# One output tile of a batched product stored by sixteen transfers in place of one

## The chip, the cores and the metric

The kernel runs on one core of a Trainium2 chip. Its time is the device time of one execution in microseconds (us), lower is better: the median of the runs before is 300.16 us. The profile is of one such execution. Five compute and control engines appear in it: PE (TensorE, matrix products), ACT (ScalarE), DVE (VectorE), POOL (GpSimd) and SP (SyncE, which here only issues transfers). Besides these there are 16 DMA engines, which move the bytes between the chip's main memory and the on-chip memory; a transfer is split over them.

## What is computed

For each of 96 (batch, head) pairs the kernel multiplies a 512 x 64 matrix by the transpose of another:

```python
x: (8, 12, 512, 64) float32
y: (8, 12, 512, 64) float32
np.einsum('bhtc,bhsc->bhts', x, y).astype(np.float32)   # (8, 12, 512, 512)
```

It reads 25.17 MB and writes 100.66 MB, so four bytes in five are results.

## The kernel before

The 96 pairs are taken in six groups of 16 (`NG`). An input of a group, 2 MB of float32, is one transfer: 128 rows (partitions) of 16 KB. There are twelve such loads (`load`, line 142), x and y in turn. The results leave in 48 output tiles (`V * NH`), each 2 MB as well: 128 partitions of `K * S` = 8 x 512 float32, which is 16 KB each. In main memory a tile is not one block: it is seen as 64 x 2 rows (`q`, `u` in the view `ov`, lines 55 to 57), two blocks of 64 rows of 16 KB; row `q` of block `u` lies in partition `2q + u`.

Loads and stores share five buffers of 2 MB, `slots`, given out in turn (`slot`, line 138). A slot that holds a result is free for the next one when its store has landed.

The inputs are turned to bfloat16 and rearranged: `compress` (line 151) copies a loaded slot on ACT, DVE and POOL, `mix` (line 174) gathers pieces of x, and `transposes` (line 189) makes the transposed operands on DVE. TensorE runs a loop over all output tiles (`all_products`, line 223); a tile is two halves of four products each, one half in each of two accumulators `pm`. `result` (line 241) copies the two halves from `pm` into a slot, on ACT for every tile but the last, and then calls `store` (line 237).

All order between engines is written out by hand. `emit` (line 113) works out which semaphores an operation has to wait for, gives the waits to its engine ahead of it, and lets the operation raise a semaphore when it is done. Each slot has a semaphore of its own for transfers (`dma0` to `dma4`); a transfer raises it by 16 in all when every part has landed. `need` (line 73) leaves out a wait that the engine has already made. Who next writes into a slot waits for the full count of the transfers that read it.

Every transfer is issued by SP, in the order of the program: first five loads, then the rest of the loads and the first stores as slots come free, and from the twelfth load on only stores. A store is issued as soon as the second half of its tile is in the slot. SP's queue is in order, so whatever stands behind an issue waits for it.

At the end of the program POOL waits for all semaphores, last of all for the last store's, and clears them.

Of the kernel before, what the change touches and what calls it, by code (L numbers as in the profile page):

```python
# [9 lines left out]
def kernel(  # L10
# [22 lines left out]
    nc = tc.nc  # L33
    B, H, T, C = x.shape
    _, _, S, _ = y.shape
# [7 lines left out]
    K = 8  # L43
    E = R // K
    D = 32
    SLOTS = 5
    fp32 = mybir.dt.float32
    bf16 = mybir.dt.bfloat16
    u32 = mybir.dt.uint32
# [5 lines left out]
    ov = out.rearrange("b h t s -> (b h t s)").rearrange(  # L55
        "(o u h q n) -> o h q u n", u=2, h=V, q=Q * E, n=K * S
    )

    def buffer(name, width, dtype):
        return nc.alloc_sbuf_tensor(name, [P, width], dtype)[:, :]  # L60

    slots = [buffer(f"slot{i}", K * S, fp32) for i in range(SLOTS)]
    xks = [buffer(f"xk{i}", R * C, bf16) for i in range(NG - 1)]
# [9 lines left out]
    def need(name, points, told=True):  # L73

        best = {}
        for p, v in points:
            if known[name].get(p, 0) < v:
                best[p] = max(best.get(p, 0), v)
        for p, v in list(best.items()):
            if any(snaps[q, w].get(p, 0) >= v for q, w in best.items() if q != p):  # L80
                del best[p]
        for p, v in best.items():
            if told:
                engines[name].wait_ge(sems[p], v)  # L84
            known[name][p] = v
            for q, w in snaps[p, v].items():
                known[name][q] = max(known[name].get(q, 0), w)

    def promise(name, reads, writes):

        points = [writer[r] for r in (*reads, *writes) if r in writer]
        points += [v for w in writes for v in readers.get(w, ())]
        if name == "pool" and name in ticks:
            points.append((name, ticks[name]))
        return points

    def record(name, p, step, reads, writes, queue=False):
        at = (p, ticks.get(p, 0) + step)
        ticks[p] = at[1]
        if not queue:  # L100
            own[name][p] = at[1]
        snaps[at] = {**known[name], **own[name], p: at[1]}
        for r in reads:
            readers.setdefault(r, []).append(at)
        for w in writes:
            writer[w], readers[w] = at, []

    def signal(p):
        if p not in sems:
            sems[p] = nc.alloc_semaphore(p)  # L110
        return sems[p]

    def emit(name, make, reads=(), writes=(), dma=None, by=None, step=1):
        need(name, promise(name, reads, writes))
        p = by or name
        if dma is not None:
            p, step = f"dma{dma}", 16
        make().then_inc(signal(p), step)
        record(name, p, step, reads, writes, dma is not None)
# [15 lines left out]
    def both(i):  # L135
        return [("slot", i, 0), ("slot", i, 1)]

    def slot():
        made_slots.append(len(made_slots) % SLOTS)
        return made_slots[-1]  # L140

    def load(n):
        i = loaded[n] = slot()
        emit(
            "sp",
            lambda: nc.sync.dma_start(slots[i], (yv if n % 2 else xv)[n // 2]),  # L146
            writes=both(i),
            dma=i,
        )
# [86 lines left out]

    def store(o, s):
        i, h = divmod(o, V)
        emit("sp", lambda: nc.sync.dma_start(ov[i, h], slots[s]), reads=both(s), dma=s)

    def result(o, s):

        ot = slots[s].rearrange("p (r s) -> p r s", s=S)
        for k in range(0, K, 4):
            pm = k // 4
            half = o // V % 2
            reads, writes = [("xT", half), ("yT", half)], [("pm", pm)]
            signal("pe")
            need("pe", promise("pe", reads, writes), told=False)
            record("pe", "pe", 1, reads, writes)  # L250
            copy(
                "dve" if o == V * NH - 1 else "act", ot[:, k:k + 4, :], pms[pm],
                [("pm", pm)], [("slot", s, pm)], by=f"free{pm}",
            )
        store(o, s)
# [9 lines left out]
    with tc.tile_critical():  # L265
        for n in range(SLOTS):
            load(n)
# [12 lines left out]
    for n in range(2 * NG):  # L280
# [6 lines left out]
        if n < 5:  # L287
            load(n + SLOTS)
        elif n in (6, 8):
# [52 lines left out]
```

## Time and profile before

| | |
|---|---|
| median of three runs | 300.16 us (300.13 to 300.43) |
| the profiled execution | 300.31 us |
| its span, first to last instruction | 298.2 us |
| transfers | 12 loads and 48 stores of 2048 KB each |
| bytes | 25.17 MB read, 100.66 MB written, 422 GB/s over the span |
| ACT busy | 208.0 us (70%) |
| DVE busy | 156.4 us (52%) |
| PE busy | 140.3 us (47%) |
| POOL busy | 56.1 us (19%) |
| SP: issue of a store | 0.54 us median, 48 of them |
| store, from issue to landing | 20.8 us median |

The page cuts the span into 40 equal slices, one digit for the busy share in tenths. "Idle before" and "waited for" name what released an engine. The chain of work that ended last is followed back from the end of the program. The trace also holds every DMA packet (start, duration, size) and every arrival at a semaphore; a packet's record doesn't say which of the 16 DMA engines moved it.

Tile 20, which the change touches, is issued as a store at 144.7 us and has landed at 165.6 us.

### The profile page before, as it was taken

How to read it: one execution, taken by the hardware profiler on the slowest of the kernel's cores; microseconds unless marked ns; L12 is line 12 of the kernel's file. 1: busy time of each engine (PE TensorE's matmuls, PEld its weight loads, DVE VectorE, ACT ScalarE, POOL GpSimd, SP SyncE). 2: the span in 40 equal slices, each digit the busy share in tenths (PEclk: the TensorE clock that was granted, in tenths of full speed). 3: DMA queues.
4: the chain of work that ended last, by engine and by line, in shares of the span. 5: the costliest groups of instructions: out<-in, count | busy, mean ns of one | idle time of the engine just before them, and what ended most of it. 6: DMA issues, size and time to landing. Idle time of an engine off the chain costs nothing.

```text
span 298.2 us, 1225 instructions
## 1 busy us (share of the span) xinstructions
PE 140.3 (47%) x384; PEld 36.5 (12%) x384; DVE 156.4 (52%) x75; ACT 208.0 (70%) x107; POOL 56.1 (19%) x23
## 2 busy tenths in 40 slices
PE   0000040548556655747566746666746656656000
PEld 0000010111111111111111111111111111111000
DVE  2257897999839592916809449076093430002300
ACT  1665576999999988686868686868676777774000
POOL 2399999991000000000000000000000000000000
PEclk9999999996799997595676595677596677596555
DMA  7999999999999999999999999999999999999996
GB/s 275 429 426 440 424 431 424 426 435 431 431 426 437 426 431 432 431 431 431 433 429 434 429 433 426 433 429 435 429 429 424 424 431 429 424 426 429 426 426 288
DMA packets 8642, 125.85 MB, mean 422 GB/s; under 512 B 960, under 2 KB 960, under 8 KB 960
## 3 DMA queue, kind: packets, MB, share of 16 engines
q1 hardware_dynamic: 8640, 125.83, 99.2%
q14 instruction: 2, 0.02, 0.0%
HBM read 25.17 MB, written 100.66 MB: 422 GB/s over the span
## 4 chain that ended last, share of the span: by engine, by line
DMA 62%; ACT 22%; issue 4%; DVE 3%; PE 1%; SPq 0%; ACTq 0%; DVEq 0%
DMA out_dram<-slot 48%; ACT slot L127 20%; DMA slot<-in_y_dram 7%; DMA slot<-in_x_dram 6%; DVE yb L129 2%; DVE slot L129 2%; PE pm L217 1%; ACT xk L127 1%; ACT yb L127 1%; SPq L146 0%; ACTq L84 0%; SPq L269 0%; DVEq L84 0%; SPq L265 0%
## 5 line engine op out<-in xcount | busy, mean ns | idle before, releaser
L217 PE MATMUL pm<-yT,xT 128*128 128x512 bf16 x384 | 140.3, 513 | 133.9 <-ACT slot L127 97.2
L127 ACT ACTIVATE slot<-pm 128x2048 f32<-128x2048 f32 x94 | 170.5, 1891 | 42.4 <-DMA out_dram<-slot 40.5
L194 DVE STREAM_TRANSPOSE xT<-xb 128x2048 uint32<-128x2048 uint32 x12 | 46.8, 3896 | 69.9 <-PE pm L217 67.5
L217 PEld LDWEIGHTS pm<-yT,xT 128*128 128x128 bf16 x384 | 36.5, 116 | 237.1 <-ACT slot L127 150.4
L129 DVE COPY xb<-xk 32x2048 bf16<-32x2048 bf16 x36 | 46.9, 1304 | 1.0
L129 DVE CAST yb<-slot 64x2048 bf16<-64x2048 f32 x12 | 36.2, 3019 | 13.1 <-DMA slot<-in_y_dram 12.9
L129 POOL COPY xb<-xk 32x2048 bf16<-32x2048 bf16 x12 | 36.2, 3020 | 6.6 <-ACT xk L127 5.9
L127 ACT ACTIVATE xk<-slot 128x4096 bf16<-128x4096 f32 x6 | 21.7, 3617 | 12.5 <-DMA slot<-in_x_dram 12.5
L203 DVE STREAM_TRANSPOSE yT<-yb 128x1024 uint32<-128x1024 uint32 x12 | 23.1, 1924 | 0.0
L129 DVE COPY slot<-pm 128x2048 f32<-128x2048 f32 x2 | 4.5, 2287 | 32.9 <-DMA out_dram<-slot 32.9
L127 ACT ACTIVATE yb<-slot 64x2048 bf16<-64x2048 f32 x6 | 14.8, 2462 | 5.1 <-DMA slot<-in_y_dram 5.1
L129 POOL CAST yb<-slot 64x2048 bf16<-64x2048 f32 x6 | 17.8, 2969 | 1.3 <-DMA slot<-in_y_dram 0.8
L127 ACT ACT_TABLE_LOAD x1 | 1.3, 1283 | 4.5 <-PEq L269 4.5
L276 DVE MEMSET xb<- 128x2048 uint32 x1 | 1.8, 1765 | 5.0 <-PEq L269 5.0
L276 POOL MEMSET xb<- 128x2048 uint32 x1 | 1.8, 1804 | 4.1 <-POOLq L269 4.1
L326 POOL MEMSET const-float32-0.0<- 128x1 f32 x1 | 0.1, 98 | 0.2 <-issue 0.2
L326 POOL MEMSET const-float32-1.0<- 128x1 f32 x1 | 0.1, 98 | 0.0
L326 POOL MEMSET const-bfloat16-1.0<- 128x1 bf16 x1 | 0.1, 98 | 0.0
L326 POOL MEMSET const-uint8-127<- 128x1 uint8 x1 | 0.1, 98 | 0.0
## 6 DMA issues: line engine op xcount, KB each, us to landing
out_dram<-slot SPq DMA_DIRECT2D x48, 2048.0 KB, 20.8
slot<-in_x_dram SPq DMA_DIRECT2D x6, 2048.0 KB, 17.5
slot<-in_y_dram SPq DMA_DIRECT2D x6, 2048.0 KB, 20.8
```

The source lines that it names most:

```text
L127: lambda: nc.scalar.activation(dst, src, COPY)
L129: else engines[name].tensor_copy(dst, src),
L194: lambda: nc.vector.transpose(xTs[half].rearrange("p (k r e) -> p k e r", k=K, e=E), xbs[half].rearrange("p (k e c) -> p k e c", k=K, e=E),),
L203: lambda: nc.vector.transpose(yTs[half].rearrange("p (r j) -> p j r", r=D), ybs[half][b].rearrange("p (j c) -> p j c", c=D),),
L217: last = nc.tensor.matmul(pms[k // 4][:, j, :], xT[:, k + j, h, :], yT[:, h * S:(h + 1) * S], start=True, stop=True,)
L276: lambda: engines[name].memset(xbs[half], 0.0),
L326: nc = _bacc.Bacc("TRN2", target_bir_lowering=False, num_devices=1)
```

## The change

```diff
+    N = K * S
+    UNEVEN = 20
...
     def store(o, s):
         i, h = divmod(o, V)
-        emit("sp", lambda: nc.sync.dma_start(ov[i, h], slots[s]), reads=both(s), dma=s)
+        if o != UNEVEN:
+            emit("sp", lambda: nc.sync.dma_start(ov[i, h], slots[s]), reads=both(s), dma=s)
+            return
+        cut = N - S
+        parts = [(ov[i, h][:, :, :cut], slots[s][:, :cut])]
+        for u, counts in enumerate(((15, 14, 13, 12, 10), (11, 9, 8, 7, 6, 5, 4, 3, 3, 8))):
+            q = 0
+            for n in counts:
+                parts.append((ov[i, h][q:q + n, u, cut:], slots[s][2 * q + u:2 * (q + n - 1) + u + 1:2, cut:]))
+                q += n
+        for dst, src in parts:
+            emit("sp", lambda: nc.sync.dma_start(dst, src), reads=both(s), dma=s)
```

47 of the 48 stores stay as they are. Tile 20 is stored by sixteen transfers, issued one after another on SP's queue where the one stood: first the leading 14 KB of all 128 rows (3584 of 4096 float32), then the last 2 KB (512 float32) of each row, by fifteen transfers. Five of them have the 64 rows of block 0, in runs of 15, 14, 13, 12 and 10 rows; ten have the 64 rows of block 1, in runs of 11, 9, 8, 7, 6, 5, 4, 3, 3 and 8. Row `q` of block `u` is read from partition `2q + u`, so a run takes every second partition. All sixteen raise the semaphore of the same slot, and the next writer of the slot waits for all of them. The bytes stored are the same, and nothing is changed on the compute engines but the count in that wait. The purpose as stated is that DMA engines of a high number move less.

## The prediction

> **What bounds the kernel now.** I read the page's DMA rows first, then the queue table, the chain, the rows of the store issue, and last the trace's packet records.
>
> ```profile
> DMA  7999999999999999999999999999999999999996
> DMA packets 8642, 125.85 MB, mean 422 GB/s; under 512 B 960, under 2 KB 960, under 8 KB 960
> q1 hardware_dynamic: 8640, 125.83, 99.2%
> DMA 62%; ACT 22%; issue 4%; DVE 3%; PE 1%; SPq 0%; ACTq 0%; DVEq 0%
> out_dram<-slot SPq DMA_DIRECT2D x48, 2048.0 KB, 20.8
> ```
>
> The 16 DMA engines are busy in every slice but the first and last: 99.2% of sixteen engines' span. No compute engine is above 70%. There are 60 transfers of 2 MB; 8,640 packets are 60 x 16 x 9, so on each DMA engine a transfer is eight rows of 16 KB and one 4-byte completion write (the 960 small ones).
>
> The chain in order of time (start, us, what) shows a loop from 126 us on:
>
> ```profile
> 129.93 20.85 DMA out_dram<-slot
> ...
> 150.86 3.65 ACT slot L127 x2
> ...
> 154.53 20.85 DMA out_dram<-slot
> ```
>
> and the timeline has the copies into the split store's slot, waiting for its landing:
>
> ```profile
> 165.64 3.65 ACT L127 ACTIVATE slot<-pm 128x2048 f32<-128x2048 f32 x2 [1.29 <-DMA out_dram<-slot]
> ```
>
> A store lands 20.85 us after its issue, ScalarE refills the slot in 3.65 us, and the store five later is issued. In 20.85 us four transfers are in the queue (20.85 / 4.92), so the DMA engines are never out of work. The loop follows them; it doesn't set their pace.
>
> What ends the span is finer than the page. The packet records (start, duration, size; no engine number) and the semaphore arrivals show sixteen streams. A 16 KB packet is recorded with 611 ns and the next begins 607 ns after it; a 4-byte one with 9 ns and the next begins 6 ns later. Fifteen streams need 8 x 607 + 6 = 4,862 ns a transfer (first arrivals 85.71 to 110.02 for five). One stream, followed back from its last packet at 297.66 to 115.84, has no gap and takes 181.82 / 37 = 4.914 us a transfer: about half of its packets take 614 to 644 ns. The arrivals of a store's sixteen completions (us) show it falling behind:
>
> ```
> store  issued   1st     15th    16th    16th after 1st
>  4      78.20   86.11   86.59   86.69   0.57
> 20     144.71  163.87  165.00  165.56   1.69
> 30     193.88  212.58  213.49  214.77   2.19
> 47     278.36  296.03  296.57  298.14   2.10
> ```
>
> The span ends at 298.2, right behind that one arrival, 1.57 us after all others. So the end is set by the sum of one DMA engine's packets. It lies in mid-field at 61 us and loses some 60 ns a transfer from there, so its slowness belongs to the engine, not to a place in the order. The trace doesn't say which number it has.
>
> **The change, part by part.** Store 20, one transfer of 128 rows x 16 KB, becomes one of 128 rows x 14 KB and fifteen with 128 pieces of 2 KB between them. By the change's description high numbers move less; I cost it so that a transfer of n rows gives a piece to each of the n lowest engines. Counting which of the fifteen sizes exceed e, engines 0 to 15 get 15, 15, 15, 13, 12, 11, 10, 9, 7, 6, 5, 4, 3, 2, 1, 0 pieces (128), where before each had eight. [...] No trace here shows it yet.
>
> Removed from every engine: 2 KB of eight packets. 14 KB is not in the trace; on the line between the 8 KB instruction packets (309 ns) and 16 KB (611) it is 309 + 302 x 6/8 = 535.5 ns, pitch 531. Saved: 8 x 76 = 0.61 us. Bounds: 0 (a fixed packet price) to 8 x 302 = 2.4 (an 8 KB price); I take the line, since two sizes lie on it.
>
> Added: a 2 KB packet and a completion write for each piece. On the line from the 32-byte packets (7 ns) to 8 KB (309), 2 KB is 82 ns, pitch 78, and 6 for the write: 84 ns. Bounds: 6 + 6 ns and 309 + 6 ns; I take 84, as 2 KB is eight times the completion's time or more by bytes alone (611 / 8 = 76). Net, by engine: 15 gains 0.61; 14, 0.52; 13, 0.44; down by 0.084 a piece to 0.02 at engine 8; engine 7 loses 9 x 84 - 608 = 0.15, engine 4 0.40, engines 0 to 2 15 x 84 - 608 = 0.65.
>
> Added on SP: fifteen issues at the same point of its queue, with no new wait on compute (all read a slot already waited for).
>
> ```profile
> L239 SPq DMA_DIRECT2D out_dram<-slot x48: 538/539/668, 54.8 to 278.4; - x48
> L146 SPq DMA_DIRECT2D slot<-in_x_dram x6: 328/358/527, 1.0 to 41.5; - x6
> ```
>
> A small issue is not in the trace; 0.33 (a load's) to 0.67 us (the longest store's) bound it, 15 x that is 4.9 to 10.1 us. SP, busy from 144.71, is free at 145.25 + 4.9 = 150.2 or at 155.3. Behind it stand store 21 (issued at 149.62 before) and, at worst, store 22 (154.53); store 23 (159.46) is not touched. For these waits ScalarE, five stores later. Cover: the fastest engine finishes store 20 at 163.9, and a packet starts 1.03 us after its issue (0.95 and 1.98 for the first load), so store 21 is in time until about 162.4. Cost nothing; without that cover each us past it is a us lost, which needs 1.14 us an issue.
>
> The extra completions raise ScalarE's wait for this slot to all sixteen transfers; that wait moves with the last engine, and ScalarE has about 1.3 us idle before each pair of copies, so nothing new queues there.
>
> Sum, if the late engine is number 15: -0.61, and all of it reaches the end, since that stream has no gap behind store 20 that could swallow it, and the next to arrive are at most 296.57 + 0.65 = 297.22, before 298.14 - 0.61 = 297.53. Against the profiled execution of 300.31 us (span 298.2, 2.1 around it) that is 299.70; against the median of 300.16, which is 0.15 less, 299.55.
>
> **Rivals.**
> (a) *The late engine is number 7.* The one late stream would get nine pieces for eight: +0.15, 300.31. For it: the trace tells no number; against: the same. [...]
> (b) *It is one of 8 to 14*: -0.02 to -0.52, 299.64 to 300.14. (c) *It is one of 0 to 6*: +0.23 to +0.65, 300.39 to 300.81. Sorted by their first packets, the streams can be followed to 61 us by their fixed spacing; the late one was then among the middle ones, not the last starter. If engines start in order of number that speaks for (b) or (c); nothing shows that they do.
> (d) *The low engines become the last, and the kernel slower.* Engines 0 to 2 alternate fifteen times between a 2 KB packet and a completion. If each pair costs more than the line says, they pass the late one. They land store 47 between 296.03 and 296.57 now; to land after 298.14 they must lose 1.57 to 2.10, that is a pair of (1.57 + 0.61) / 15 = 0.145 to 0.18 us. At 0.21 a pair they lose 2.5: 300.5 to 301.1; at the 8 KB bound, 4.1: 302.1 to 302.7. For it: completions arrive 0.4 to 0.5 us after their packet, and never were so close together. Against: after a completion the next packet begins 6 ns later in all 60 transfers.
> (e) *The pieces spread evenly, against the description.* Eight pieces each: 8 x 84 - 608 = +0.06, 300.22.
>
> **How the numbers follow.** Likeliest, engine 15, no more than a choice by the trace: 0.52; its own range is 299.4 to 299.8, from 0.1 of spread in times and small prices either way. (a) 0.10, (b) 0.10, (c) 0.12, (d) 0.12, (e) 0.04. A difference of 0.2%, 0.60 us, is about what a measurement of this kernel tells from none. The forecast lies just past that bound; I count two thirds of 0.52 as faster (0.34), because the stream's own 4.914 / 8 = 0.614 a packet, with its interruptions, is slightly more than the line's. Slower: (d) 0.12, and engines 0 to 2 from (c), 0.08. The rest, 0.46, is no change. The range 299.3 to 300.9 takes in the likeliest, (a), (b), (c), (e) and the mild end of (d), and leaves some 0.16 out.
>
> **What would show it.** Right: the sixteenth arrival of store 20 comes about 0.6 us sooner against the store before it, and the last store's 1.57 us gap to the fifteenth shrinks below 1.0; the page counts 16 x 9 packets of store 20 replaced by 16 x 9 + 2 x 128, so 8,896 on the queue. SP's issues at the split take 5 to 10 us and no DMA slice falls below 9. Wrong: the late stream's packets of store 20 include 2 KB ones (then (a) to (c), and their count names the engine), or pairs above 0.145 us (d), or first arrivals of store 21 late with idle streams before them (the cover).

## The result: slower by half a per cent, and the profile after

The changed kernel takes 301.75 us (median of five, 301.6 to 302.17) against 300.32 before; the ratio is 1.0053, 95% interval 1.0038 to 1.0067. The forecast was 299.55, with a range of 299.3 to 300.9. The profiled execution took 301.70 us with a span of 299.9, that of before 300.31 with 298.2.

The rows of its page that answer to those shown above: the DMA engines' busy share, the bytes per second in the 40 slices, the packets, and the chain.

```profile
DMA  7999999999999999999998999999999999999998
GB/s 271 428 433 433 426 426 439 424 422 422 441 431 422 439 431 423 437 433 424 437 431 355 392 420 420 420 441 433 420 420 422 440 428 422 420 439 428 426 420 352
DMA packets 8899, 125.86 MB, mean 420 GB/s; under 512 B 1088, under 2 KB 1088, under 8 KB 1216
q1 hardware_dynamic: 8896, 125.83, 99.0%
DMA 57%; ACT 20%; SPq 7%; issue 4%; DVE 3%; PE 1%; ACTq 0%; DVEq 0%
```

Two slices of 7.5 us, the 22nd and 23rd, moved 355 and 392 GB/s where the slices before them moved some 430; against 430 that is (75 + 38) x 7.5 / 430 = 2.0 us of standing still. SP's queue, nothing in the chain before, now has 7% of it. The chain in order of time (start, us, what) shows where:

```profile
140.98 3.65 ACT slot L129 x2
...
144.65 0.54 SPq L252
145.19 0.04 issue
145.23 1.45 SPq L252
146.68 0.05 issue
146.73 1.32 SPq L252
...
160.76 1.42 SPq L252
...
163.39 0.66 SPq L252
...
164.09 0.68 SPq L252
164.78 0.04 issue
164.82 0.60 SPq L242
165.42 0.04 issue
165.47 10.98 DMA out_dram<-slot
```

Line 252 is the loop over the parts. Its first issue takes 0.54 us like any store's, the next twelve 1.3 to 1.45 us each. Store 21, whose tile was in its slot at 149.6, is issued at 164.82, and its first packets start at 166.07. Busy time in stretches (length, engines, then granted clock, DMA share and GB/s at the end of the row) shows the gap:

```profile
155.00:162.00 7.00, 3.64 (x11) 0.82 (x9) 6.32 (x3) 4.90 (x3) 0.00 (x0) 0.75 0.99 422
162.00:166.20 4.20, 3.52 (x8) 0.86 (x8) 4.11 (x4) 2.39 (x2) 0.00 (x0) 0.50 0.67 251
```

and the kernel before has none there:

```profile
162.00:166.00 4.00, 2.64 (x8) 0.69 (x8) 3.93 (x4) 2.71 (x3) 0.00 (x0) 0.83 1.00 426
```

In 162 to 166.2 a third of the DMA engines' time was idle. All sixteen streams then begin store 21 between 166.07 and 166.22 us, whatever they had to move before. The sixteenth arrivals, which ended the span before, tell what of it reached the end:

```
sixteenth arrival, us    store 19   store 21   store 47   19 to 21   21 to 47
before                    160.62     170.49     298.14       9.87     127.65
after                     160.66     171.62     299.80      10.96     128.18
```

The two differences, 1.09 and 0.53, with 0.04 that was there before the split, make the 1.66 us by which the last arrival is later. The first difference is the split and the dry queue behind it. The second arises in a place where the two programs are alike; it is a step of about 0.6 us at 235 us.

The packet records hold 128 packets of 14 KB and 128 of 2 KB for tile 20. The 2 KB ones took 84 ns and followed each other, with a completion between, every 86 ns; the 14 KB ones took 535 ns. They can be strung to sixteen streams with 15, 15, 15, 13, 12, 11, 10, 9, 7, 6, 5, 4, 3, 2, 1 and 0 pieces. The late stream of store 19, followed on, has twelve. The trace has no engine numbers; if the lowest ones take part in a small transfer, as the prediction had it, the late stream is engine number 4, and it is called so below.

### The profile page after: what moved, and what is told of

It reads as the page before. It is cut to its first block, busy times and chain, and to the rows that moved or that the text cites. A ratio compares the mean times of both kernels' runs of the same rounds, so it can differ in the third digit from the quotient of the medians.

```text
span 299.9 us, 1240 instructions
## 1 busy us (share of the span) xinstructions
PE 140.4 (47%) x384; PEld 36.2 (12%) x384; DVE 156.4 (52%) x75; ACT 208.0 (69%) x107; POOL 56.0 (19%) x23
## 2 busy tenths in 40 slices
DMA packets 8899, 125.86 MB, mean 420 GB/s; under 512 B 1088, under 2 KB 1088, under 8 KB 1216
## 3 DMA queue, kind: packets, MB, share of 16 engines
q1 hardware_dynamic: 8896, 125.83, 99.0%
## 4 chain that ended last, share of the span: by engine, by line
DMA 57%; ACT 20%; SPq 7%; issue 4%; DVE 3%; PE 1%; ACTq 0%; DVEq 0%
DMA out_dram<-slot 44%; ACT slot L129 18%; DMA slot<-in_y_dram 7%; SPq L252 6%; DMA slot<-in_x_dram 6%; DVE yb L131 2%; DVE slot L131 1%; PE pm L219 1%; ACT xk L129 1%; ACT yb L129 1%; SPq L148 0%; SPq L242 0%; ACTq L86 0%; SPq L282 0%; DVEq L86 0%
```

## The experiments

Theory A: SP's issues cost more than was priced, so that store 21 came after the queue had run dry. Theory B: the pieces and their completions cost it on the DMA engines. The shorter names C to F are told where they come up.

**The same pieces by ten transfers.** 15 rows eight times and 4 rows twice, so that SP falls less behind.

```diff
-        for u, counts in enumerate(((15, 14, 13, 12, 10), (11, 9, 8, 7, 6, 5, 4, 3, 3, 8))):
+        for u, counts in enumerate(((15, 15, 15, 15, 4), (15, 15, 15, 15, 4))):
```

> Tile 20 is stored by eleven transfers in place of sixteen: 14 KB of every row, then eight of 15 rows and two of 4 rows, the same 128 pieces of 2 KB. Theory A (SP's issues back to back cost 1.4 us each, outlast what is queued, and the DMA engines run dry): SP is free at 144.7 + 0.5 + 10 x 1.4 = 159.4, store 21 is in time (before about 162.4), no DMA slice under 9 in the middle. The late engine, if it is one of 4 to 14, gets 8 pieces, +0.06; if it is 15, -0.61. Time 300.2 to 300.6, or 299.7. Theory B (the small transfers themselves cost it: pieces and completions on the DMA engines): the pieces are as many, so the loss stays, 301.4 to 301.8.

Measured 300.88 us, ratio 1.0022 (1.0013 to 1.0031): less than half of the loss. Store 21 was issued at 158.97 and no engine went idle for it. Theory B, by which the loss of 1.4 stays, did not expect that; A did; but 0.6 us is more than the 0.06 that A leaves, and 300.88 lies above A's range.

**The sixteen transfers in another order.** Eight small ones, two stores, then the other seven.

```diff
...
-        for dst, src in parts:
+        for dst, src in parts[:9]:
             emit("sp", lambda: nc.sync.dma_start(dst, src), reads=both(s), dma=s)
+        late.append((parts[9:], s))        # issued behind store 22
```

> The sixteen transfers of the changed kernel, all of them, in another order on SP: the 14 KB one and eight small ones, then the stores of tiles 21 and 22, then the other seven small ones. Theory A: store 21 is issued at 145.2 + 8 x 1.4 = 156.4, the DMA engines never run dry, and only the pieces are left: the late engine, which got 12 pieces in the changed kernel, loses 12 x 0.086 - 0.61 = 0.4. Time 300.4 to 300.9. The slot of tile 20 comes free some 5 to 8 us later, which delays one tile on ScalarE but is covered by the queue. Theory B: no better than the changed kernel, 301.4 to 302.

Measured 301.45 us, ratio 1.0039 (1.0025 to 1.0052): above A's range and at B's. Its slices show no gap (424, 426, 428 and 425 GB/s from 150 to 180 us), so the dry queue is gone, and something else costs. Its sixteenth arrivals take 10.06 us from store 19 to 21 and 128.64 from 21 to 47, which is +0.19 and +0.99 (another 0.56 us of its last arrival was there at store 19 already; the profile is of the slowest of its five executions). The late stream has eight of the first eight pieces, so it is one of engines 0 to 7, as engine 4 would be. For that engine 12 x 0.086 - 0.61 = 0.42 is explained, and 0.76 not: again mostly a step of 0.6, at 234 us.

**Sixteen transfers of 1 KB of every row.** As many issues, but all on 16 engines alike. Theory C: only transfers on fewer than 16 engines have slow issues.

```diff
...
+        w = N // 16
+        for c in range(16):
+            emit("sp", lambda: nc.sync.dma_start(ov[i, h][:, :, c * w:(c + 1) * w], slots[s][:, c * w:(c + 1) * w]), reads=both(s), dma=s)
```

> Tile 20 is stored by sixteen transfers that each have 1 KB of all 128 rows, so every one runs on all 16 DMA engines and none gets more than another. Theory A (any issue right behind another costs 1.4 us while the DMA engines are busy): SP is free at 144.7 + 0.5 + 15 x 1.4 = 166.5, later than in the changed kernel by 1.7 us; idle DMA engines for 3 to 4 us; 302.3 to 303.5. [...]

Measured 301.52 us, ratio 1.0043 (1.0027 to 1.0058). The row of the line (duration in ns, least, median, most):

```profile
L246 SPq DMA_DIRECT2D out_dram<-slot x16: 539/1376/1600, 144.7 to 163.8; - x16
```

The first took 539 ns and the next twelve 1.28 to 1.60 us, with all sixteen engines in each: C falls. The loss is smaller than A's number, since the last three took 0.6 us, as in the changed kernel: an issue right behind another was slow while the DMA engines had work, and quick once they had run dry. Store 21 was thus issued at 164.44 and not at 166.5.

**The split at tile 8.** Where less is queued.

```diff
-    UNEVEN = 20
+    UNEVEN = 8
```

> The changed kernel with the split at tile 8 in place of tile 20, where less is queued: store 8 is issued at 92.7 and the DMA engines have work until about 105. Theory A: SP is free at 92.8 + 0.5 + 20.1 = 113.4, first packets of store 9 at 114.6, so the DMA engines stand idle for 9 us; less the lag of the late engine, about 1: 307.5 to 309.5. Theory B: the same pieces cost the same anywhere, 301.4 to 302.

Measured 304.97 us, ratio 1.0157 (1.0142 to 1.0173): three times the loss from the same pieces, so B falls as the main cause. The number was too high: SP was free at 109.0 and not 113.4, because here too the issues became quick (0.63 to 0.90) when the engines ran dry.

```profile
GB/s 272 430 430 432 424 432 428 426 424 437 428 430 435 376 214 414 430 435 417 428 435 416 439 424 417 441 422 417 441 424 417 440 419 419 441 422 419 443 419 348
```

The gap is in the slices that begin at 98 and 106 us (376 and 214), right where the queue of tile 8 ends.

**Only a longer program on SP.** The step at 233 to 258 us in the runs so far stands beside an 8 KB packet of the instruction queue that the kernel before doesn't have in its span. Theory D: it is SP's, pulled in by the added instructions. The kernel before with fifteen instructions on SP that move nothing:

```diff
         emit("sp", lambda: nc.sync.dma_start(ov[i, h], slots[s]), reads=both(s), dma=s)
+        if o == 20:
+            for _ in range(15):
+                emit("sp", nc.sync.nop)
```

> The kernel before, with fifteen instructions on SP behind store 20 that only raise a semaphore of SP's own; no transfer is changed. Theory D (in the changed kernel and the experiments so far SP's longer program pulled one more 8 KB instruction fetch into the span, at 234 us with fifteen instructions more and 258 us with ten; it stands in the late engine's queue and lengthens its lag by 0.58 us): a fetch at about 234 us, the sixteenth arrival later by 0.6 from there on, 300.28 + 0.58 = 300.7 to 301.0. Rival E (the fetch is hidden, and what the e1 kernel lost came from its pieces): 300.1 to 300.4.

Measured 300.69 us, ratio 1.0013 (1.0004 to 1.0022). The packet rows of its page:

```profile
DMA packets 8643, 125.86 MB, mean 421 GB/s; under 512 B 960, under 2 KB 960, under 8 KB 960
q1 hardware_dynamic: 8640, 125.83, 99.0%
q14 instruction: 3, 0.02, 0.0%
```

The transfers' 8,640 packets are those of before; there is one more packet of 8 KB, an instruction fetch at 232.8 us. The sixteenth arrival's lag behind the first goes from 2.15 to 2.72 us there and stays near that. D holds: its price is 0.4 us in the median, a hair under its range, and 0.6 in this profile; E's range ends at 300.4.

**Two halves.** One instruction more.

```diff
...
+        for c in (slice(0, 2048), slice(2048, 4096)):
+            emit("sp", lambda: nc.sync.dma_start(ov[i, h][:, :, c], slots[s][:, c]), reads=both(s), dma=s)
```

> The kernel before with store 20 as two transfers of 8 KB of all 128 rows: one SP instruction more, the same bytes on every DMA engine. The second issue right behind the first: 1.4 us (theory A), 0.54 otherwise; either way hidden. Theory D: fetches came at the 61st transfer that SP issues (12 loads, 15 small and 34 stores; 12, 10 and 39), so with one transfer more the fetch comes with the last store's issue at 278 us, is inside the span, and if it is the late engine that does it, 300.6 to 301.0. Rival E: 300.1 to 300.4.

Measured 300.25 us, ratio 0.9997 (0.9988 to 1.0006): no change. The second half's issue took 1.39 us: the price of A by itself, hidden. The fetch came at 300.5, behind the end, so the count in the expectation was wrong. Set beside the profiles so far it is SP's 66th transfer: in the four kernels with 75 of them and the one with 70 the fetch stands within 0.6 us of the 66th issue (234.5 and 234.3 us in the changed kernel, 258.0 and 258.0 in the one with 70); with 60 or 61 transfers and no idle instruction it comes after the end. The fifteen idle instructions count like transfers: with them the 66th is SP's 51st transfer, at 233.4 us, and that fetch stands at 232.8.

**Relief for engine 4, from ScalarE's queue.** Four transfers of 4 rows go to engines 0 to 3, so that the others move less.

```diff
...
+        emit("sp", lambda: nc.sync.dma_start(ov[i, h][:48], slots[s][:96]), reads=both(s), dma=s)
+        parts = [(ov[i, h][48:, 0], slots[s][96::2]), (ov[i, h][48:, 1, :1536], slots[s][97::2, :1536])]
+        for q in range(48, 64, 4):
+            parts.append((ov[i, h][q:q + 4, 1, 1536:], slots[s][2 * q + 1:2 * q + 8:2, 1536:]))
+        for dst, src in parts:
+            emit("act", lambda: nc.scalar.dma_start(dst, src), reads=both(s), dma=s)
```

> Tile 20 in seven transfers, one on SP (96 rows, six per DMA engine) and six on ScalarE's queue, so that SP's program is no longer than before: 16 rows one to an engine, 6 KB of the last 16 rows one to an engine, and the other 10 KB of these by four transfers of 4 rows, which go to engines 0 to 3. These get 3 x 10 KB more, the other twelve 10 KB less (0.38 us). By its 12 pieces the late engine of the changed kernel was number 4. If it is 4 or higher here: the last arrival comes 0.38 sooner, 299.8 to 300.1. If it is one of 0 to 3: 1.1 later, 301.2 to 301.6. If ScalarE's six issues (1.4 us each, 8.4 in all) starve the queue: 302 or more.

Measured 304.36 us, ratio 1.0128 (1.0112 to 1.0143). ScalarE's issues and the stretches:

```profile
L247 ACTq DMA_DIRECT2D out_dram<-slot x6: 640/1646/1860, 144.6 to 152.2; - x6
...
148.00:160.00 12.00, 3.69 (x9) 1.08 (x11) 0.00 (x0) 5.92 (x4) 0.00 (x0) 0.57 1.01 393
160.00:168.00 8.00, 4.83 (x20) 1.34 (x17) 5.43 (x2) 8.00 (x5) 0.00 (x0) 1.00 1.00 336
```

The DMA share stays at 1.0 while the bytes fall to 393 and 336 GB/s: not an empty queue, but longer packets: of the 436 of 16 KB that begin from 148 to 168 us, 100 last over 0.65 us, up to 1.77, in place of 0.61. The time lies in the range given for a starved queue, but not by that cause. The small transfers did not stand behind the queued stores, as on SP's queue (issued from 145.23 us, first packet at 163.13 in the changed kernel), but beside them: the first ran at 148.96 us. The run says nothing on which engine is late.

**Relief from SP's queue, and its control.** Six transfers each; the control moves the same 5 KB of the last 32 rows evenly.

```diff
...
+        cut = K * S - 1280
+        parts = [(ov[i, h][:, :, :cut], slots[s][:, :cut]), (ov[i, h][:48, :, cut:], slots[s][:96, cut:])]
+        for q in range(48, 64, 4):
+            parts.append((ov[i, h][q:q + 4, :, cut:], slots[s][2 * q:2 * q + 8, cut:]))
...
+        # control, in place of the loop over q:
+        for c in range(cut, K * S, 640):
+            for u in range(2):
+                parts.append((ov[i, h][48:, u, c:c + 640], slots[s][96 + u::2, c:c + 640]))
```

> Tile 20 in six transfers, all on SP, that give the engines from 4 up less: 11 KB of all 128 rows, 5 KB of 96 rows, and 5 KB of the last 32 rows by four transfers of 8 rows that go to engines 0 to 3, two rows each. Engines 4 to 15 move 2 x 5 KB less (0.38 us), engines 0 to 3 6 x 5 KB more (1.1 us). SP is free at 144.7 + 0.5 + 5 x 1.4 = 152.2, in time. The extra instruction fetch comes with SP's 66th transfer, of which there are 65: outside the span, or with what SP does right after its last issue at 278 us (then + 0.4). If the late engine is one of 4 to 15 (12 pieces in the changed kernel: number 4): 299.8 to 300.1, with the fetch 300.2 to 300.5. If it is one of 0 to 3: 301.2 to 301.9. By the theory that the late engine has to do with high numbers the same as for 4; the next run tells what the form costs.

> The control to the run before: the same cut, also six transfers, but the 5 KB of the last 32 rows go out as four transfers of 16 rows x 2.5 KB, one to each engine, so that all 16 engines move as much as in the kernel before. Nothing but 16 more packets and 5 more completions on each engine: 300.2 to 300.6, and 0.38 above the relief kernel if the late engine is one of 4 to 15.

Relief 301.27 us, ratio 1.0039 (1.0025 to 1.0053); control 300.62, ratio 1.0011 (1.0002 to 1.0020). The fetch fell inside both spans, at 284 and 283 us. In the relief kernel the late stream of store 19 has none of the extra pieces (it is 4 or higher) and does gain, but engines 0 to 3 are the last from store 21 on: fifteenth and sixteenth arrival stand 3.07 and 3.22 us behind the first. They lost more than the 1.1 us of their bytes, since 32 of the 128 pieces of 5 KB lasted over 40 ns longer than the usual 196. The control's slice beside the split dips like the relief's (406 and 400 GB/s), and its time is only 0.11% up. So both expectations failed: 301.27 falls in the range given for a late engine of 0 to 3, but through those engines and not through the late one, and the control, at 300.62 just above its range, is faster than the relief and not 0.38 slower. No version here beats the kernel before.

**The late issue alone.** No small transfer, no piece, no extra fetch; SP only waits for the landing of store 20 before it issues store 21. Theory F: idle time is made good later.

```diff
+        if o == 21:
+            p = f"dma{made_slots[-2]}"
+            need("sp", [(p, ticks[p])])
         emit("sp", lambda: nc.sync.dma_start(ov[i, h], slots[s]), reads=both(s), dma=s)
```

> The kernel before, all stores whole, with one wait more: SP issues store 21 only when store 20 has landed (about 165.6 in place of 149.6), as late as the changed kernel did (164.8). No small transfer, no gradient, and one SP instruction more, too few for the extra instruction fetch. Theory A (what the changed kernel lost is above all the dry queue): the fifteen other engines stand idle for some 3 us, the late one for 1.3 to 1.7; its lag of 1.7 us is gone at store 21 (sixteenth arrival within 0.4 us of the first); the end is later by what the late engine stood idle, 301.4 to 302.0. Theory F (the idle time is made good later, as the loop has slack, and the changed kernel lost by its pieces and the fetch): 300.2 to 300.7.

Measured 301.79 us, ratio 1.0052 (1.0038 to 1.0065). What SP waited for, the stretch of the gap, and the bytes:

```profile
SPq L242 <- DMA out_dram<-slot: 15.9, 1, 15.9
...
162.00:166.00 4.00, 3.35 (x8) 0.87 (x8) 3.91 (x4) 2.79 (x3) 0.00 (x0) 0.57 0.40 172
...
GB/s 275 426 431 437 422 431 428 431 424 433 437 424 431 437 424 429 439 426 428 437 426 357 350 420 420 431 437 426 420 420 435 435 424 420 424 439 426 424 420 385
```

One wait of 15.9 us, store 21 at 165.42 us, two slices with 357 and 350 GB/s, and a loss as large as the changed kernel's, without its pieces and its fetch, but with store 21 issued another 0.60 us later. F falls.

## Why the prediction was wrong, step by step

The sixteenth arrivals of eight kernels put the terms side by side (us; the last column is where the fetch stands):

```
                         19 to 21   21 to 47   extra fetch
before                      9.87     127.65    no
halves                      9.88     127.68    no
late issue alone           11.65     127.58    no
fifteen idle instructions   9.84     128.26    232.8 us
ten small transfers        10.06     128.23    258.0 us
control of the relief      10.00     128.23    283.2 us
sixteen of 1 KB            10.55     128.11    234.1 us
changed kernel             10.96     128.18    234.5 us
```

Without a fetch the second column is 127.58 to 127.68, with one 128.11 to 128.26. So the last arrival lost 0.5 to 0.6 us beside the fetch in every kernel of the table that had it. The other four kernels are left out, since other transfers or another last stream decide their columns. One of them looks like an exception: the split at tile 8 has a fetch at 237.8 us and still 127.41 in the second column. The sixteenth arrival's lag grows there too, from 0.39 to 0.97 us; but its last stream at store 21 had been put back 0.8 us beside another fetch at 166 us, and had made that good by then.

In the table the first column grows past 10.1 only where SP was late, and there it follows the issue of store 21: over the kernel before it is 0.68 us more with the issue at 164.44, 1.09 at 164.82 and 1.78 at 165.42, about a us for each us past 163.7. The first of these kernels has even pieces, the second uneven ones and the third none, so this column is the late issue's, whatever the pieces.

- *What bounds the kernel: right as far as the runs show.* Before and after the change the end follows one DMA engine's sum, and what its last arrival lost is found in that engine's packets, its fetch or its idle time; in the relief from SP's queue engines 0 to 3 took its place. The pace of 4.862 us for the others holds only until about 205 us: from there on most of them take 4.91 like the late one, and in the three kernels of the table whose queue ran dry all sixteen do right after it. A limit that all engines share from then on is not excluded.
- *"A small issue ... 0.33 (a load's) to 0.67 us (the longest store's) bound it": this is the step that failed.* It is 1.3 to 1.45 us right behind another issue while the DMA engines have work, so SP was busy with the sixteen for 20.1 us. The rows I bounded it by were of issues with a pause ahead of them, or of the first five loads (0.39 to 0.63 us, issued from 0.95 to 3.00), when the first packets, at 1.98, had hardly begun. The text gave the point from which it decides, 1.14 us an issue, and left it outside the bounds, so the dry queue got no chance of its own. The rest of that reckoning stood: store 21 had to be issued by about 162.4, was issued at 164.82, and the first packets came 1.25 us later (1.03 was taken). That each us past the limit is a us lost held as well, but from 163.7 us on, since 162.4 is the limit of the fastest engine, which first had its lead to lose. The kernel that only issues store 21 late shows that a late issue alone can cost as much. Of the 1.66 us by which the changed kernel's last arrival is later, 1.09 belong to this step and 0.53 to the stretch with the fetch.
- *The late engine as number 15: wrong, a choice without a row.* By its twelve pieces, counted from the lowest number, it is number 4, case (c), worth 12 x 0.086 - 0.61 = +0.42 by the packets' own times and not -0.61. Three other runs agree as far as they can: one of 0 to 7, one of 4 to 14, and 4 or higher. Nor is it the number 7 of case (a), which by the same count has nine; number 15 has none. That the streams with more pieces are the lower numbers was the author's assumption, which no trace shows. This error did not decide the time: since all sixteen streams begin store 21 within 0.15 us, a late engine with fewer pieces would have waited longer and gone on at the same moment. Number 15 could have gained only with store 21 in time.
- *Nothing for the longer program: a term left out.* One more 8 KB instruction fetch costs about 0.4 us in the median (the fifteen idle instructions: 0.13% of 300.3 is 0.39, interval 0.1 to 0.7).
- *The price of pieces: right.* 84 ns a piece was forecast and 86 measured, 535 for the 14 KB packet was both, and 8,896 packets on the queue were forecast and found. Rival (d), low engines slowed by pairs above 0.145 us, didn't come about in the changed kernel.
- *How the transfers spread: right as far as a trace without engine numbers can tell.* The sixteen streams have the forecast counts of pieces; that they follow the engines' numbers is not shown, so the -0.61 for number 15 was an assumption, and the stream of the last arrival had twelve pieces and not none. The semaphore of that slot has 335 arrivals: 12 x 16, 128 for the pieces, and 15 more, one for each small transfer. For these 15 there is no packet: the queue has 1,088 completions of 4 bytes, and the five slots' semaphores 1,103 arrivals. Twelve of the 15 came by 162.60 us, each 0.38 to 0.42 us after the end of its issue and before any part of store 20 had landed (163.48 the first). What raises the semaphore for them is not shown.
- *The signs.* The gap of the last store's sixteenth arrival to the fifteenth did shrink below 1.0 us, to 0.49, but because the others had lost their lead and not because the late stream had gained: a sign that two causes share tells neither. Of the other signs the packet count held, but SP's issues took 20.1 us and not 5 to 10, and a slice in the middle of the DMA row fell to 8. Two of the signs of being wrong came: the late stream of store 20 had 2 KB packets, and store 21 arrived late behind idle streams.

In the changed kernel's trace the late stream's +1.09 divides into its 12 pieces (0.42) and its idle time (0.67), but the sum of the two is set by the issue of store 21. The other engines stood still longer: the first arrival of store 21 is 2.64 us later than before, the sixteenth 1.13. The difference of 1.5 us is the lead that the first had had, and that was worth nothing.

## What to carry to other kernels

A transfer added beside a full queue is paid on the issuing engine: here about 1.4 us for each issue right behind another while the DMA engines had work, for 4 rows of 2 KB (1.42) as for 128 rows of 8 KB (1.39). Count issues times that against what is queued, and don't price it from issues that had a pause before them (0.54). When all DMA engines are busy to the end, look for the one that arrives last: idle time of the others was free here as far as they were ahead (of the first arrival's 2.64 us, 1.5), its own was not, and neither was an instruction fetch beside its packets that a longer program on SP brought (0.5 to 0.6 us).

## What the runs showed of the hardware that was not expected

- The issue of a store took 0.54 us after a pause. Right behind another, while the DMA engines had work, it took 1.29 to 1.45 us in the changed kernel, 1.28 to 1.60 in the one with sixteen of 1 KB, and 1.65 in the median of the six on ScalarE's queue; 4 rows of 2 KB took 1.42 and 128 rows of 8 KB 1.39. As the DMA engines ran dry it took 1.12 and then 0.60 to 0.68 in the changed kernel and 0.63 to 0.90 with the split at tile 8. What the engine waits for in it is not shown.
- SP's instruction fetch is 8 KB in 0.31 us, came with its 66th transfer, or behind the last of 65, and put 0.5 to 0.6 us on the last arrival in each kernel of the table that had it: the packet's own time, and most of the rest in the 16 KB packet behind it, which took 0.77 to 0.89 us in place of 0.61.
- The completions of the small transfers came late: the last one of store 20 arrived at 167.33 us, 1.7 us behind the end of its last packet, where the kernel before shows 0.4 to 0.5 us.
- Transfers from a second engine's queue ran beside the queued ones, and the sixteen engines fell to 336 GB/s in eight microseconds with a busy share of 1.0.
- After the queue had run dry, the late stream kept within 0.35 us of the first to the end in the kernel that only issues late; all sixteen then took 4.91 us a transfer, where before fifteen had taken 4.86 until about 205 us. Its own pace was 4.91 in both. Why engine 4 is late, and why the others give up their lead, stays open.
